# Row-tiled gate matmuls, casting weight loads and an accumulated low part in the recurrent block of a two-layer trunk

## The chip, the cores and the metric

The kernel runs on one core of one Trainium2 chip. The metric is the device time of one execution in microseconds (us), and lower is better. A difference of about 0.2%, here 3.1 us, is what a measurement of this kernel can tell from no change.

## The reference

Two layers work on x, 512 positions by 1024 features, all in float32. Each layer adds half a SwiGLU block, then a mixer, then half a second SwiGLU block; RMSNorm stands ahead of each. The second layer's mixer is a spatial gating unit. The change touches the first layer's mixer alone, the recurrence:

```python
def recurrent_mixer(x, w_in, conv_w, conv_b, gate_a_w, ..., lam, w_out):
    y, r = jnp.split(x @ w_in, 2, axis=-1)          # w_in: 1024 x 2048
    y = jax.nn.gelu(y)
    r = causal_depthwise_conv(r, conv_w, conv_b)    # width 4
    h = rg_lru(r, ...)
    return (y * h) @ w_out                          # w_out: 1024 x 1024

def rg_lru(x, w_a, b_a, w_x, b_x, lam):
    gate_a = sigmoid(block_diag_linear(x, w_a, b_a))   # 16 heads of 64 x 64
    gate_x = sigmoid(block_diag_linear(x, w_x, b_x))
    log_a = -8 * gate_a * softplus(-lam)
    a = exp(log_a)
    bx = x * gate_x * sqrt(-expm1(2 * log_a))
    return associative_scan(a_l * a_r, a_r * b_l + b_r)  # h[t] = a[t] h[t-1] + bx[t]
```

## The kernel before

**Products.** Every matrix product that needs float32 precision is made of three single-pass products in the type fp32r: each operand is split into a high part (the value rounded to fp32r, made by a copy on ScalarE, named `hi` or `whi`) and a low part (value minus high part, made by a subtraction on VectorE, `lo` or `wlo`); high x high, low x high and high x low are summed in PSUM. So one 128x1024 weight tile costs ScalarE one copy and VectorE one subtraction, and TensorE 24 matmuls of 512 columns or their like.

**Steps.** The program is a list of steps (`subs`); a step is one weight tile: its load, its split, its matmuls. A hand-made loop at the end of the kernel emits the steps in order. At each step it emits the split of the tile that is used three steps later (`SPLIT_AHEAD`), then work hooked to this step, in the phases "pre", "mid" and "rest", then as many further weight loads as fit into 10 buffers (`load_more`, `RAW_BUFS`), then the step's matmuls, then hooks of the phases "end" and "late". Every engine runs its own instructions strictly in the order of emission and waits where an operand isn't ready. SyncE's queue carries plain loads; GpSimd's queue carries loads that add onto what is in the buffer.

**The recurrent block.** Features lie on partitions and the 512 positions along the free dimension. It has 20 steps ahead of its output product:

- Eight half steps and four full ones make r, 128 features (c = 0 to 7) at a time. When the last matmul of c is done, `r_post` hooks its work: ScalarE copies r out of PSUM with the conv's last tap, VectorE adds three taps (`taps`), the result `rc` is split (ScalarE `hi`, VectorE `lo`), TensorE makes the gates (`gate`, line 1237 on), ScalarE the two sigmoids out of PSUM and a tanh (`sigmoids`).
- Gates: the 64x64 blocks of two heads stand on the diagonal of a 128x128 weight that is zero elsewhere, one weight for gate a and one for gate x; three matmuls of 128 rows by 512 columns each, so six for one c and 48 in all (lines 248 to 250, tile `gate`).
- Eight full steps make y, 24 matmuls of 512 columns each, with r and y weight tiles 128x8x128 of `rec_w_in`. Meanwhile `plan` sets exp, sqrt, the scan and gelu on ScalarE and VectorE for c = 0 to 4 and then 5 to 7.
- Then the output product, steps of 12 matmuls (tiles A, B, C), reads y*h, which is split like every other left operand. Its `rec_w_out` tiles get sums of blocks by adding loads on GpSimd's queue.

TensorE's matmuls are listed with the weight loads (LDWEIGHTS, engine PEld) that belong to them one for one.

Of the kernel before, what the change touches and what calls it, by code (L numbers as in the profile page):

```python
# [9 lines left out]
F32R = mybir.dt.float32r  # L10
# [4 lines left out]
P = 128  # L15
# [19 lines left out]
RAW_BUFS = 10  # L35
SPLIT_AHEAD = 3
SLOTS = 56
V_AT = 1, 7, 9, 10
WS_AT, WS_MERGE = 90, 8

# [35 lines left out]
def trunk(ctx: ExitStack, tc: tile.TileContext, a: dict, out: bass.AP):  # L76
# [57 lines left out]
    class Raw:  # L134


        halves = False
# [7 lines left out]

        def load(self):
            _, k, c = self.shape
            t = rawp.tile([P, 1024], F32, tag="raw", name=nm("raw"))
            self.v = t[:, : k * c].rearrange("p (k c) -> p k c", k=k)
            live.add(self)  # L150
            self.fetch()
            if self.plus is not None:
                pending.append((now[0] + self.wait, self))
                pending.sort(key=lambda p: p[0])
# [3 lines left out]
                nc.sync.dma_start(out=self.v[:, q, :], in_=self.src[:, q, :])  # L158
# [15 lines left out]
    class Sub:  # L174
# [19 lines left out]
        def split(self, between=None):  # L194

            if self.hi is not None:
                return
            self.add()
            src = self.raw.v
            assert self.tile is None and self.raw.plus is None and self.raw.done == self.at[0]  # L200
# [12 lines left out]
            self.raw.used()  # L213
# [989 lines left out]
    def recurrent(w_in, w_out, norm):  # L1203
        gates = {}

        def load_gate(name, q):
            g = gates[name, q] = slot(name="gw")
            nc.gpsimd.memset(g, 0.0)
            gv = g.rearrange("p (c j) -> p c j", c=4)
            wv = a[f"rec_gate_{name}_w"][0, q * 8 : (q + 1) * 8].rearrange("(c two) i j -> two i c j", two=2)  # L1210
            for two in range(2):
                nc.sync.dma_start(out=gv[two * 64 : (two + 1) * 64, :, two * 64 : (two + 1) * 64], in_=wv[two])

        def split_gate(name, q):
            gates[name, q] = split(gates[name, q])

        at0 = len(subs)
        y0 = at0 + 12
        for n, (name, q) in enumerate((name, q) for q in range(2) for name in ("a", "x")):
            hook(at0 + (-9,-8,-2,-1)[n], "late", lambda name=name, q=q: load_gate(name, q))  # L1220
            hook(at0 + (-3,-2,3,4)[n], "mid", lambda name=name, q=q: split_gate(name, q))

        rc, ga, gx, tl, pr, ym = {}, {}, {}, {}, {}, {}

        def r_post(c, ps):
            n = now[0]
            g = n + (2 if c < 4 or c == 6 else 1)
            v = rc[c] = slot(name="rc")
            hl, pss = [], []
            act(v, ps, AF.Identity, scale=vcol(V_CW + 24 + c), bias=vcol(V_CB + c))  # L1230

            def taps():
                for k in (0, 1, 2):
# [23 lines left out]
            hook(n + 1, "mid", lambda: hl.extend(split(v)))  # L1257
# [57 lines left out]
        plan(1, "late", (exp_, 5, 6, 7), (oma2, 5, 6, 7))  # L1315
        plan(2, "rest", (sqrt, 5, 6, 7))
        plan(2, "late", (gelu, 0, 1, 2), (scan, 5, 6, 7))
# [25 lines left out]
        def mk(c0, post, halves):  # L1343

            raw = raw_of(w_in[:, c0 : c0 + P].rearrange("(k p) c -> p k c", p=P), [P, KD, P])
            st = {}
# [10 lines left out]
            last = lambda: post(st[0])  # L1357
# [310 lines left out]
    def vec_rest():  # L1668

        nc.vector.memset(stage[:V_ROWS, :P], 0.0)  # L1670
        for src, r0, n in rows:
            flat = src.rearrange("h d -> (h d)") if len(src.shape) == 2 else src.rearrange("o h d -> (o h d)")
            nc.gpsimd.dma_start(out=stage[r0 : r0 + n, :P], in_=flat.rearrange("(n p) -> n p", p=P))

    def vec_rest_t():
        ps = aux("vec")
# [146 lines left out]
```

## Time and profile before

| | us |
|---|---|
| median of 3 runs (1559.05 to 1560.93) | 1559.81 |
| the profiled execution | 1559.84 |
| its span, first to last instruction | 1557.0 |
| r steps and the first gates (328.2 to 397.5 of the span, y steps from 383.9 on) | about 69 |
| y steps up to the output product | ends at 430.1 |

The granted TensorE clock is 0.999 over the span. The profiled execution lies 0.03 us from the median, so the sum can be made against it. A row of the timeline reads: start, duration, engine, line, operation, output<-inputs, shapes; in brackets stands idle time of the engine just before, and what ended it. A matmul's duration contains its way through the array, so rows overlap, and the distance from one start to the next is what a matmul takes from TensorE.

### The profile page before, as it was taken

To read this page: it belongs to the slowest core of one execution; us is meant where nothing else is said; L and a number is where in the kernel's file an instruction comes from. 1 tells how busy PE (TensorE), PEld (TensorE's weight loads), DVE (VectorE), ACT (ScalarE), POOL (GpSimd) and SP (SyncE) were. 2 spreads that over 40 slices of the span, in tenths; PEclk is the share of its full clock that TensorE was granted. 3 is DMA by queue.
4 is the path that set the end of the run, shared out by engine and by line. 5 is a ranking of instruction groups with operands and counts; after the bars stand their busy time and mean duration, and the time that the engine had idled before them with its cause. 6 is when DMAs were issued, how large, how long until landed. Compare 5 with 4: busy or idle time off the path is not lost.

```text
span 1557.0 us, 20941 instructions
## 1 busy us (share of the span) xinstructions
PE 1549.4 (100%) x7237; PEld 1314.8 (84%) x7237; DVE 1310.5 (84%) x1792; ACT 1197.0 (77%) x1789; POOL 245.6 (16%) x220
## 2 busy tenths in 40 slices
PE   9999999999999999999999999999999999999998
PEld 7888888898888998888889988888888889888886
DVE  6977789888999787789897877798879997777998
ACT  7877786668778868786787787867887877777866
POOL 2111112300021111112211211122111111111120
PEclk9999999999999999999999999999999999999999
DMA  9988898953395988899987898989978869898994
GB/s 315 189 189 194 187 219 225 225 146 108 99 235 136 190 199 198 186 237 217 233 212 181 201 219 184 223 229 236 233 200 212 203 141 218 195 210 180 242 234 135
DMA packets 275098, 312.09 MB, mean 200 GB/s; under 512 B 117568, under 2 KB 155568, under 8 KB 274992
## 3 DMA queue, kind: packets, MB, share of 16 engines
q1 hardware_dynamic: 220704, 211.59, 47.6%
q0 software_dynamic: 52496, 97.33, 36.9%
q10 hardware_dynamic: 1792, 1.84, 0.4%
q8 instruction: 56, 0.92, 0.2%
q14 instruction: 50, 0.41, 0.1%
HBM read 282.39 MB, written 2.10 MB: 183 GB/s over the span
## 4 chain that ended last, share of the span: by engine, by line
PE 98%; DVE 1%; DMA 1%; issue 0%; ACT 0%; SPq 0%
PE A L484 15%; PE A L483 15%; PE A L485 15%; PE C L483 8%; PE C L485 8%; PE C L484 8%; PE B L484 4%; PE B L485 4%; PE B L483 4%; PE r L248 2%; PE r L250 2%; PE r L249 2%; PE Q L483 1%; PE Q L485 1%; PE Q L484 1%; PE p L963 1%
## 5 line engine op out<-in xcount | busy, mean ns | idle before, releaser
L110 DVE TENSOR_TENSOR wlo<-raw,whi 128x1024 fp32r<-128x1024 f32 (+2 forms) x567 | 651.1, 1152 | 208.8 <-ACT whi L119 203.6
L119 ACT ACTIVATE whi<-raw 128x1024 fp32r<-128x1024 f32 (+2 forms) x567 | 564.3, 1001 | 226.8 <-DVE raw L110 91.6
L483 PE MATMUL A<-whi,hi 128*128 128x512 f32 (+1 forms) x1104 | 420.9, 381 | 0.0
L484 PE MATMUL A<-whi,lo 128*128 128x512 f32 (+1 forms) x1104 | 419.4, 380 | 0.1
L485 PE MATMUL A<-wlo,hi 128*128 128x512 f32 (+1 forms) x1104 | 419.2, 380 | 0.0
L484 PEld LDWEIGHTS A<-whi,lo 128*128 128x128 f32 x1104 | 207.3, 188 | 36.0 <-DVE lo L110 1.0
L483 PEld LDWEIGHTS A<-whi,hi 128*128 128x128 f32 x1104 | 207.2, 188 | 36.0 <-ACT c L119 1.0
L485 PEld LDWEIGHTS A<-wlo,hi 128*128 128x128 f32 x1104 | 207.2, 188 | 35.6
L483 PE MATMUL C<-whi,hi 128*128 128x512 f32 (+1 forms) x608 | 231.5, 381 | 0.0
L484 PE MATMUL C<-whi,lo 128*128 128x512 f32 (+1 forms) x608 | 231.4, 381 | 0.0
L485 PE MATMUL C<-wlo,hi 128*128 128x512 f32 (+1 forms) x608 | 231.3, 380 | 0.0
L161 POOL DMA_DIRECT2D raw<-in_ffn_w_in_dram x100 | 120.7, 1207 | 697.4 <-DVE raw L110 331.5
L161 POOL DMA_DIRECT2D raw<-in_ffn_w_out_dram x73 | 83.8, 1195 | 318.3 <-DVE wlo L110 203.3
L110 DVE TENSOR_TENSOR raw<-raw,raw 128x1024 f32<-128x1024 f32 (+1 forms) x113 | 130.9, 1158 | 1.1
L484 PEld LDWEIGHTS C<-whi,lo 128*128 128x128 f32 x608 | 114.1, 188 | 20.4 <-DVE lo L110 0.4
L485 PEld LDWEIGHTS C<-wlo,hi 128*128 128x128 f32 x608 | 114.1, 188 | 19.9
L483 PEld LDWEIGHTS C<-whi,hi 128*128 128x128 f32 x608 | 114.1, 188 | 19.9
L110 DVE TENSOR_TENSOR lo<-a,hi 128x512 fp32r<-128x512 f32 (+1 forms) x180 | 116.3, 653 | 0.7 <-ACT hi L119 0.7
L119 ACT ACTIVATE c<-A 128x512 f32<-128x512 f32 (+1 forms) x150 | 81.8, 567 | 45.6 <-PE A L485 45.3
L119 ACT ACTIVATE hi<-a 128x512 fp32r<-128x512 f32 (+1 forms) x180 | 105.4, 595 | 14.4 <-DVE a L110 12.8
L484 PE MATMUL B<-whi,lo 128*128 128x512 f32 (+1 forms) x304 | 115.7, 381 | 0.1
L483 PE MATMUL B<-whi,hi 128*128 128x512 f32 (+1 forms) x304 | 115.7, 381 | 0.0
(189 smaller groups left out, 1974.0 us busy)
## 6 DMA issues: line engine op xcount, KB each, us to landing
raw<-in_ffn_w_in_dram SPq DMA_DIRECT2D x143, 512.0 KB, 5.6
raw<-in_ffn_w_out_dram SPq DMA_DIRECT2D x98, 512.0 KB, 6.0
raw<-in_ffn_w_in_dram POOLq DMA_DIRECT2D x76, 512.0 KB, 7.5
raw<-in_ffn_w_out_dram POOLq DMA_DIRECT2D x58, 512.0 KB, 8.6
raw<-in_ffn_w_in_dram SPq DMA_DIRECT2D x48, 384.0 KB, 4.3
raw<-in_sg_w_in_dram SPq DMA_DIRECT2D x20, 512.0 KB, 9.0
raw<-in_ffn_w_in_dram POOLq DMA_DIRECT2D x24, 384.0 KB, 6.2
raw<-in_rec_w_in_dram SPq DMA_DIRECT2D x16, 512.0 KB, 5.1
```

Source lines behind the costliest of these rows:

```text
L110: nc.vector.tensor_tensor(out=o, in0=x, in1=y, op=op)
L119: nc.scalar.activation(out=o, in_=x, func=f, **k)
L161: nc.gpsimd.dma_start(out=self.v, in_=src, accum_op=ALU.add)
L248: nc.tensor.matmul(ps, wh, xh, start=start, stop=False)
L249: nc.tensor.matmul(ps, wh, xl, start=False, stop=False)
L250: nc.tensor.matmul(ps, wl, xh, start=False, stop=stop)
L483: nc.tensor.matmul(ps, zh, wh, start=fresh and i == 0, stop=False, **k)
L484: nc.tensor.matmul(ps, zl, wh, start=False, stop=False, **k)
L485: nc.tensor.matmul(ps, zh, wl, start=False, stop=end, **k)
L963: nc.tensor.matmul(bank_of(half, s), z, (sub.lo if m == 2 else sub.hi)[:, q, :], start=left[2] == "2" and (h, q, m) == (0, 0, 0), stop=lef ...
```

## The change

1. **Gates by row tiles.** One weight of 128 partitions x 128 columns holds gate a and gate x: partitions 0 to 63 hold [a | x] of the first head, partitions 64 to 127 hold [x | a] of the second. A gate's matmul reads 64 partitions and writes 128 PSUM partitions; per c there are still six, three for each half of the partitions, alternating between the halves, and each half has its own PSUM bank. There are two weights in place of four, so two splits in place of four, and no zero fill on GpSimd.
2. **Sigmoids.** Each bank now holds one head's a and x, so a sigmoid covers 64 partitions: four for each c in place of two. The bias of gate x is loaded with its halves swapped (one more small load at the start).
3. **Later gates.** The gates of a c stand 3 or 2 steps after its `r` (`GATE`) where they stood 2 or 1 steps after; c = 2 and 3 come at one place, all others alone. Before, c = 3 and 4 came at one place, and c = 6 and 7. exp, sqrt and the scan move by up to one step.
4. **Casting loads.** For r's c = 4 to 7 and y's c = 0 to 5 the high part is loaded from memory by a load on GpSimd's queue that casts to fp32r (`rawhi`), beside the plain load; ScalarE's copy of these ten tiles goes. Each such tile holds two of the 10 buffers, so loads run fewer tiles ahead.
5. **Accumulated low part.** For y's c = 6 and 7 there is no plain load: ScalarE writes minus the high part to a second buffer (`rawlo`), and an adding load of the same weights onto it makes the low part. VectorE's two subtractions go.
6. **Conv parts.** The high part of `rc` for c = 4 to 7 is a copy on VectorE.

```diff
+GATE = (3, 3, 3, 2, 2, 2, 2, 2)
+OWN_HI = 4
+BELOW = {6: 2, 7: 2}
...
         def load(self):
             _, k, c = self.shape
+            if self.below:
+                self.h, self.l = (rawp.tile([P, 1024], F32R, tag="raw", ...) ... for x in ("rawhi", "rawlo"))
+                live.update(((self, "hi"), (self, "lo")))
+                nc.gpsimd.dma_start(out=self.h, in_=self.src)
+                pending.append((now[0] + self.below, self))
...
+            if self.cast:
+                self.h = rawp.tile([P, 1024], F32R, tag="raw", name=nm("rawhi")).rearrange("p (k c) -> p k c", k=k)
+                live.add((self, "hi"))
+                nc.gpsimd.dma_start(out=self.h, in_=self.src)
...
         def add(self, src):
+            if self.below:
+                act(self.l, f32(self.h), AF.Copy, scale=-1.0)
+                nc.gpsimd.dma_start(out=self.l, in_=self.src, accum_op=ALU.add)
+                return
...
+            if self.raw.cast:
+                self.hi = self.raw.h
+                ...
+                tt(self.lo, src, f32(self.hi), ALU.subtract)
+                self.raw.used()
+                return
...
-            g = n + (2 if c < 4 or c == 6 else 1)
+            g = n + GATE[c]
...
             def gate():
-                for name in "ax":
-                    pg = bank("gate")
-                    wh, wl = gates[name, c // 4]
-                    cs = slice((c % 4) * P, (c % 4 + 1) * P)
-                    mm3(pg, wh[:, cs], wl[:, cs], hl[0], hl[1], True, True)
-                    pss.append(pg)
+                pss.extend(bank("gate") for _ in range(2))
+                cs = slice((c % 4) * P, (c % 4 + 1) * P)
+                for m in range(3):
+                    for two in range(2):
+                        rows = slice(two * 64, (two + 1) * 64)
+                        nc.tensor.matmul(pss[two], gates[c // 4][m == 2][rows, cs], hl[0][m == 1][rows, :],
+                                         start=m == 0, stop=m == 2)
...
             def sigmoids():
-                for dst, brow in ((ga, V_GA), (gx, V_GX)):
-                    dst[c] = slot(name="g")
-                    act(dst[c], pss.pop(0), AF.Sigmoid, bias=vcol(brow + c))
+                for dst, brow, n in ((ga, V_GA, 0), (gx, V_GX, 1)):
+                    g = dst[c] = slot(name="g")
+                    for two in range(2):
+                        o = (two ^ n) * 64
+                        act(g[two * 64 : (two + 1) * 64], pss[two][o : o + 64], AF.Sigmoid, bias=vcol(brow + c)[o : o + 64])
...
+                if c < OWN_HI:
+                    act(hi, v, AF.Copy)
+                else:
+                    nc.vector.tensor_copy(hi, v)
+                tt(lo, v, f32(hi), ALU.subtract)
...
-        plan(-2, "rest", (exp_, 0, 1, 2, 3, 4), (oma2, 0, 1))
+        plan(-1, "rest", (exp_, 0, 1, 2, 3, 4), (oma2, 0, 1))
...
-        while loaded < n and len(live) < RAW_BUFS:
+        while loaded < n and len(live) < RAW_BUFS - raws[loaded].cast:
```

On TensorE, around the gates of c = 0, the kernel before has (`gate` is the PSUM bank, first operand the weight, second what streams):

```order
L250 MATMUL r_3267<-zh_3086,wlo_3179 128x256
L248 MATMUL gate_3463<-hi_3394,hi_3112 128x512
L249 MATMUL gate_3463<-lo_3395,hi_3112 128x512
L250 MATMUL gate_3463<-hi_3394,lo_3113 128x512
L248 MATMUL gate_3467<-hi_3394,hi_3134 128x512
L249 MATMUL gate_3467<-lo_3395,hi_3134 128x512
L250 MATMUL gate_3467<-hi_3394,lo_3135 128x512
L248 MATMUL r_3332<-zh_3058,whi_3209 128x256
```

and the changed kernel has, one half step later:

```order
L279 MATMUL r_3323<-zh_3082,wlo_3201 128x256
L1273 MATMUL gate_3481<-hi_3379,hi_3110 128x512
L1273 MATMUL gate_3482<-hi_3379,hi_3110 128x512
L1273 MATMUL gate_3481<-lo_3380,hi_3110 128x512
L1273 MATMUL gate_3482<-lo_3380,hi_3110 128x512
L1273 MATMUL gate_3481<-hi_3379,lo_3111 128x512
L1273 MATMUL gate_3482<-hi_3379,lo_3111 128x512
L277 MATMUL r_3512<-zh_3054,rawhi_2936 128x512
```

The count is the same; the two banks alternate, and the gates stand between the last half step and the first full one.

On GpSimd's queue, where the kernel before has four zero fills and then adding loads of `rec_w_out`, the changed kernel has, after eight more rows of the kind of the first two:

```order
L166 DMA rawhi_3642<-in_rec_w_in_dram 128x8x128
L166 DMA rawhi_3713<-in_rec_w_in_dram 128x8x128
L155 DMA rawhi_3783<-in_rec_w_in_dram 128x8x128
L155 DMA rawhi_3846<-in_rec_w_in_dram 128x8x128
L178 DMA rawlo_3784<-in_rec_w_in_dram 128x8x128
L178 DMA rawlo_3847<-in_rec_w_in_dram 128x8x128
L180 DMA raw_3910<-in_rec_w_out_dram 128x2x512 x2
L180 DMA raw_4048<-in_rec_w_out_dram 128x2x512
```

So the adding load of y's last low part (`rawlo_3847`) is followed on its queue by those of `rec_w_out`.

On ScalarE, at the end of the recurrence (`gate` to `g` is a sigmoid, `tl` a sqrt, `y` a gelu), the changed kernel has:

```order
L122 ACTIVATE tl_3835<-tl_3835 128x512
L122 ACTIVATE tl_3894<-tl_3894 128x512
L122 ACT_TABLE_LOAD
L122 ACTIVATE y_3940<-r_3786 128x512
L122 ACTIVATE y_3942<-r_3849 128x512
L122 ACTIVATE y_3944<-r_3912 128x512
L122 ACTIVATE rawlo_3847<-rawhi_3846 128x1024
L122 ACTIVATE hi_3992<-a_838_3959 128x512
```

The kernel before has the same three gelus there, followed by the `whi` copy of y's c = 6. What moved in is the negated copy for y's c = 7, which can't start before the gelus are through.

More of the change, by code (lines that the diff above doesn't have):

```diff
@@ L147, in load @@
             _, k, c = self.shape
+            if self.below:
+                self.h, self.l = (rawp.tile([P, 1024], F32R, tag="raw", name=nm(x)).rearrange("p (k c) -> p k c", k=k)
+                                  for x in ("rawhi", "rawlo"))
+                live.update(((self, "hi"), (self, "lo")))
+                nc.gpsimd.dma_start(out=self.h, in_=self.src)
+                pending.append((now[0] + self.below, self))
+                pending.sort(key=lambda p: p[0])
+                return
             t = rawp.tile([P, 1024], F32, tag="raw", name=nm("raw"))
@@ L198, in split @@
             self.add()
+            if self.raw.below:
+                self.hi, self.lo = self.raw.h, self.raw.l
+                return
             src = self.raw.v
+            if self.raw.cast:
+                self.hi = self.raw.h
+                _, k, c = src.shape
+                self.lo = wp.tile([P, 1024], F32R, tag="wlo", name=nm("wlo")).rearrange("p (k c) -> p k c", k=k)
+                tt(self.lo, src, f32(self.hi), ALU.subtract)
+                self.raw.used()
+                return
             assert self.tile is None and self.raw.plus is None and self.raw.done == self.at[0]
@@ L1204, in recurrent, with load_gate, split_gate @@
         gates = {}
[L1206 to L1208 removed]
+        def load_gate(q):
+            g = gates[q] = slot(name="gw")
             gv = g.rearrange("p (c j) -> p c j", c=4)
[L1210 to L1215, printed above, removed]
+            for n, name in enumerate("ax"):
+                wv = a[f"rec_gate_{name}_w"][0, q * 8 : (q + 1) * 8].rearrange("(c two) i j -> two i c j", two=2)
+                for two in range(2):
+                    o = (two ^ n) * 64
+                    nc.sync.dma_start(out=gv[two * 64 : (two + 1) * 64, :, o : o + 64], in_=wv[two])
+        def split_gate(q):
+            gates[q] = split(gates[q])
         at0 = len(subs)
         y0 = at0 + 12
[L1219 to L1221 removed]
+        for q in range(2):
+            hook(at0 + (-9, -2)[q], "late", lambda q=q: load_gate(q))
+            hook(at0 + (-3, 3)[q], "mid", lambda q=q: split_gate(q))
         rc, ga, gx, tl, pr, ym = {}, {}, {}, {}, {}, {}
@@ L1345, in mk @@
             raw = raw_of(w_in[:, c0 : c0 + P].rearrange("(k p) c -> p k c", p=P), [P, KD, P])
+            raw.cast = not halves
+            raw.below = BELOW.get(c0 // P, 0)
             st = {}
@@ L1355, in mm_of, with last @@
                 return mm
-            last = lambda: post(st[0])
+            def last():
+                live.difference_update(((raw, "hi"), (raw, "lo")))
+                post(st[0])
             if not halves:
@@ L1672, in vec_rest @@
             flat = src.rearrange("h d -> (h d)") if len(src.shape) == 2 else src.rearrange("o h d -> (o h d)")
-            nc.gpsimd.dma_start(out=stage[r0 : r0 + n, :P], in_=flat.rearrange("(n p) -> n p", p=P))
+            v = flat.rearrange("(n p) -> n p", p=P)
+            if r0 == V_GX:
+                for o in (0, 64):
+                    nc.gpsimd.dma_start(out=stage[r0 : r0 + n, o : o + 64], in_=v[:, 64 - o : 128 - o])
+            else:
+                nc.gpsimd.dma_start(out=stage[r0 : r0 + n, :P], in_=v)
     def vec_rest_t():
```

17 lines of the change are left out of this document (12 added, 5 removed).

## The prediction

> **What bounds the kernel now.** I read the page first: its engines and its chain.
>
> ```profile
> span 1557.0 us, 20941 instructions
> PE 1549.4 (100%) x7237; PEld 1314.8 (84%) x7237; DVE 1310.5 (84%) x1792; ACT 1197.0 (77%) x1789; POOL 245.6 (16%) x220
> ...
> PE 98%; DVE 1%; DMA 1%; issue 0%; ACT 0%; SPq 0%
> ```
>
> TensorE is busy throughout and carries 98% of the chain. Next the view by stretches: r's full steps and y up to 430.1, then the output product.
>
> ```profile
> 356.60:397.50 40.90, 40.90 (x182) 33.87 (x182) 35.15 (x47) 34.71 (x50) 2.41 (x2) 1.00 0.41 104
> 397.50:430.10 32.60, 32.60 (x145) 27.03 (x144) 31.24 (x46) 23.13 (x33) 3.20 (x3) 1.00 0.35 98
> 430.10:470.00 39.90, 39.90 (x189) 33.28 (x188) 37.69 (x52) 29.09 (x50) 8.88 (x8) 1.00 0.94 223
> ```
>
> The columns are the stretch, its length, then PE, PEld, DVE, ACT and POOL, clock, DMA share, GB/s. TensorE never stops here, at a granted clock of 1.00. So a microsecond taken from VectorE, ScalarE or DMA buys nothing by itself; only TensorE's own work, or a new wait of TensorE, changes the time. VectorE, with 31.24 of 32.60 us, is the engine nearest to making it wait.
>
> **Change part by part. Gates on TensorE.** The first gate in the timeline:
>
> ```profile
> 350.95 0.40 PE L248 MATMUL gate<-hi,hi 128*128 128x512 f32 x1
> 351.18 0.40 PE L249 MATMUL gate<-lo,hi 128*128 128x512 f32 x1
> ...
> 352.33 0.28 PE L248 MATMUL r<-zh,whi 128*128 128x256 f32 x1
> ```
>
> Six matmuls take 352.33 - 350.95 = 1.38 us, 0.23 each. Eight gates are 8 x 1.38 = 11.0 us. After, two half-height matmuls on different partitions can run side by side. If they do, a gate streams three times 0.23 = 0.69 us, and 24 x 0.23 = 5.5 us go. No row has two side by side; the bounds are 0 and 5.5, and I take 5.5, since they share neither rows of the array nor a bank.
>
> What entering and leaving the other shape costs, one place shows: near the start a transpose of 8 rows stands between full-height warm-up matmuls, which start 0.42 us apart there, at about half the later pace.
>
> ```profile
> 1.67 1.91 PE L1660 MATMUL warm<-warm 128*128 128x512 bf16 x4
> 3.51 0.27 PE L1665 MATMUL vec<-ident,first_gain 8*128 8x8 f32 x1
> ...
> 2.10 0.15 PEld L1660 LDWEIGHTS <-warm 128*128 128x128 bf16 x1 [0.28 <-issue]
> 2.52 0.15 PEld L1660 LDWEIGHTS <-warm 128*128 128x128 bf16 x1 [0.28 <-issue]
> 3.51 0.18 PEld L1665 LDWEIGHTS vec<-ident,first_gain 8*128 8x128 f32 x1 [0.84 <-issue]
> 3.71 0.13 PEld L1660 LDWEIGHTS <-warm 128*128 128x128 bf16 x2
> ...
> 22.11 0.87 PE e L294 x8
> ```
>
> Full-height weight loads start one matmul early (2.10, 2.52: 0.42 apart, the stream of one matmul). The fourth warm-up matmul starts at 1.67 + 3 x 0.42 = 2.93 and has streamed by 3.35; the small weight load starts only at 3.51, and the next full one only at 3.71. So weights aren't loaded ahead across the change of shape, and the round trip took 3.71 - 3.35 = 0.36 us with next to nothing streamed, plus the second weight load. At full pace I halve it, 0.18, and add 0.11 for that load (eight transposes, each with its load, took 0.87): 0.29; unhalved it is 0.47. I take 0.33, near the halved end, because the array's part goes with its pace. The second half's weights come 0.11 us after the first's, which staggers the end: 0.11 more. There are seven places after (c = 2 and 3 share one): 7 x 0.44 = 3.1 us; bounds 0 (no drain, no stagger) and 7 x 0.58 = 4.1.
>
> Net on TensorE: -5.5 + 3.1 = **-2.4 us**, from -5.5 to -1.4 where the halves pair.
>
> The Trainium skill, "TensorEngine Tiling (Array Packing)", section "Key Properties", says that changing the tiling mode drains TensorE; the trace agrees in this one place (0.36 us at half the pace). The Trainium skill, "TensorE: Matmul & The Clock Gate", section "Part 3: Packing small matmuls — row/col tiling", has packed matmuls start about 4 ns apart; no run here shows it, and by it the stagger of 0.77 us in all would go, giving -3.1.
>
> **ScalarE.** Its timeline over one round, and the gelus at the end:
>
> ```profile
> 359.08 1.06 ACT L119 ACTIVATE whi<-raw 128x1024 fp32r<-128x1024 f32 x1
> 360.03 1.27 ACT L119 ACTIVATE g<-gate,vec 128x512 f32<-128x512 f32 x2
> 361.17 0.74 ACT L119 ACTIVATE tl<-g,lru_c 128x512 f32<-128x512 f32 x1
> 361.78 0.65 ACT L119 ACTIVATE hi<-rc 128x512 fp32r<-128x512 f32 x1
> 362.33 0.78 ACT L119 ACTIVATE rc<-r,vec 128x512 f32<-128x512 f32 x1
> ...
> 410.44 1.58 ACT L119 ACTIVATE y<-r 128x512 f32<-128x512 f32 x3
> ```
>
> A sigmoid costs (361.17 - 360.03) / 2 = 0.57, a `whi` 0.95, a `hi` 0.55. A 64-partition sigmoid streams as many columns, so I price it like a full one (bounds 0.29 and 0.57). Up to the three gelus: 16 more sigmoids +9.1, ten `whi` copies -9.5, four `hi` -2.2, one negated copy +0.95: -1.7 us. So the gelus end not at 410.44 + 1.58 = 412.0 but near 410.3; as the gates come later I allow 411 +- 2, and the negated copy for y's last tile ends near **412**.
>
> **The accumulated low part, the edit with a wait.** That copy releases the adding load; TensorE needs its result in the y step of c = 7:
>
> ```profile
> 425.14 0.39 PE L250 MATMUL r<-zh,wlo 128*128 128x512 f32 x1
> ...
> q0 software_dynamic: 816, 1.57, 8.4%
> ...
> raw<-in_rec_w_out_dram SPq DMA_DIRECT2D x10, 512.0 KB, 3.9
> raw<-in_rec_w_in_dram SPq DMA_DIRECT2D x8, 512.0 KB, 4.1
> raw<-in_rec_w_out_dram POOLq DMA_DIRECT2D x5, 512.0 KB, 7.4
> ```
>
> (DMA view, 318 to 430.) First use of this low part is at 425.14, after the change 425.1 - 2.4 = 422.7. Adding loads land in 7.4 us, but with rows of 2 KB; these have 512 bytes, four times the packets. On the plain queue that costs 0.2 us (4.1 against 3.9). On the adding queue a packet takes 8.4% x 16 x 112 us / 816 = 0.18 us of an engine; if small ones took as long, 768 more on 16 engines add 8.9. Bounds 7.6 and 16.3; I take 9, nearer the plain rows because the bytes are the same. 412 + 9 = 421: 1.7 us to spare, cost 0; without that cover up to 412 + 16.3 - 422.7 = 5.6 us of TensorE waiting. Behind it on GpSimd's queue stand the `rec_w_out` additions; their readers have the slack of three steps.
>
> **VectorE, the loads.** VectorE loses two subtractions of 1.2 us and two gate splits and gains four one-input copies, whose nearest row is 0.48, at most a subtraction's 0.68:
>
> ```profile
> L110 DVE TENSOR_TENSOR wlo<-raw,whi 128x1024 fp32r<-128x1024 f32 x453 | 550.8, 1220 | 164.1 <-ACT whi L119 158.9 <-DMA raw<-in_sg_w_out_dram 3.6
> L113 DVE TENSOR_SCALAR xn<-x,rt 128x512 f32<-128x512 f32 x6 | 2.6, 482 | 0.1
> ...
> 439.77 0.68 DVE L110 TENSOR_TENSOR lo<-a,hi 128x512 fp32r<-128x512 f32 x1
> 441.23 0.39 PE L484 MATMUL C<-whi,lo 128*128 128x512 f32 x1
> ```
>
> In the y stage that is 4 x 0.48 - 2.4 = -0.5 us or, at 0.68, +0.3. The tightest meeting behind it has 441.23 - 440.45 = 0.8 us, and an earlier TensorE uses this up; so a gain far over 2.4 us would partly turn into waiting here. At 2.4 I put it at nothing, and up to 2 us if nothing on VectorE moves up.
>
> Twelve casting loads and two adding ones bring some 6 MB more into these stretches at 98 to 104 GB/s, where the next one runs at 223 without stopping TensorE: nothing. GpSimd has the time (2.4 and 3.2 us busy in these stretches). `rec_w_out`'s first load moves:
>
> ```profile
> 357.60 64.13 SPq L158 DMA_DIRECT2D raw<-in_rec_w_out_dram  x10
> ```
>
> from 357.6, some 70 us before its use at 430.1, to three steps (of 24 x 0.23 = 5.5 us) before its split, against 3.9 to land: hidden.
>
> **The sum.** -2.4 + 0 + 0 on the profiled execution's 1559.84, which equals the median within 0.03: **1557.4 us**.
>
> **Rivals.**
>
> *A, the shapes change without a drain.* For it: the delay was seen once, at half the pace, in a warm-up that nothing hurried. Against: the weight loads at 3.51 and 3.71 themselves. Then only the stagger stays, -5.5 + 0.8 = -4.7 (1555.1), and c = 7's low part, needed at 420.4, lands at 421, so some 0.4 comes back: 1555.5.
>
> *B, the halves don't run together.* For it: no row shows two matmuls overlapping by more than their way through the array. Then nothing is saved and the seven round trips are paid, 7 x 0.33 = +2.3, up to 7 x 0.47 = +3.3: about 1562.5, slower. It decides whatever else holds, as soon as the second half's start comes 0.23 us after the first's.
>
> *C, the adding load comes late.* Its place is y's c = 7; it decides from a landing after 422.7, that is over 10.7 us or a ScalarE over 2 us behind my reckoning. At 16.3 us it costs 5.6: 1559.8 - 2.4 + 5.6 = 1563.0; in the middle 1560. For it: only a guess stands for small adding packets. Against: the plain rows.
>
> **Chances.** Forecast (-1.4 to -3.5) 0.42, A 0.28, B 0.12, C 0.18. Within 0.2% (3.1 us) is what a measurement of this kernel can't tell from no change. Faster by more: nearly all of A (0.27) and a seventh of the forecast (0.06): 0.33. Slower by more: over half of B (0.07) and of C (0.10): 0.17. Same: 0.50. The forecast's own range is 1556.3 to 1558.4; to hold 8 in 10 it goes down into A, 1554.6, and up through most of C and half of B, 1562.3.
>
> **What would show it.** In the profile after: the second half's matmul of a gate starts at most 0.12 us after the first's, and the six take about 0.8 us where they took 1.38 (else B). The gap from the last full-height matmul to the first gate and back adds some 0.3 us (none: A). ScalarE's gelus end at 411 +- 2. The last `rawlo` lands within 10 us and TensorE doesn't wait in y's c = 7 (else C). TensorE is first to reach the output product, near 427.7. A wait of TensorE on a conv part (`hi` or `lo` of `rc`), a gate's bank or a `rawhi` would prove my cover wrong.

## The result

| | us |
|---|---|
| before, median of 6 runs (1558.81 to 1560.93) | 1559.06 |
| after, median of 6 runs (1570.06 to 1576.33) | 1570.90 |
| forecast | 1557.4 (1554.6 to 1562.3) |

The changed kernel takes 1.0078 times as long, 95% interval 1.0064 to 1.0093: some 12 us slower, outside the range. Its profiled execution took 1570.06 us with a span of 1568.2, 11.2 us longer than the span before.

### The profile page after: what moved, and what is told of

Read it like the earlier page. It is cut to its first block, busy times and chain, and to the rows that moved or that the text cites. A ratio compares the mean times of both kernels' runs of the same rounds, so it can differ in the third digit from the quotient of the medians.

```text
span 1568.2 us, 20979 instructions
## 1 busy us (share of the span) xinstructions
PE 1549.4 (99%) x7237; PEld 1310.0 (84%) x7237; DVE 1308.7 (83%) x1792; ACT 1196.3 (76%) x1789; POOL 256.9 (16%) x231
## 3 DMA queue, kind: packets, MB, share of 16 engines
q10 hardware_dynamic: 1792, 1.84, 0.5%
## 4 chain that ended last, share of the span: by engine, by line
PE 69%; DVE 2%; DMA 1%; issue 1%; ACT 0%; POOL 0%; DVEq 0%; POOLq 0%; ACTq 0%
PE A L513 12%; PE A L512 12%; PE A L514 12%; PE C L513 7%; PE C L514 7%; PE C L512 7%; PE B L513 3%; PE B L512 3%; PE B L514 3%; PE Q L513 1%; PE Q L512 1%; PE Q L514 1%; DMA raw<-in_rec_w_out_dram 1%; PE e L323 1%; DVE wlo L113 1%
## 5 line engine op out<-in xcount | busy, mean ns | idle before, releaser
L113 DVE TENSOR_TENSOR wlo<-raw,whi 128x1024 fp32r<-128x1024 f32 (+2 forms) x555 | 636.4, 1150 | 222.0 <-ACT whi L122 215.7
L122 ACT ACTIVATE whi<-raw 128x1024 fp32r<-128x1024 f32 (+2 forms) x555 | 551.6, 1000 | 243.3 <-DVE raw L113 93.1
L514 PE MATMUL B<-wlo,hi 128*128 128x512 f32 (+1 forms) x304 | 115.7, 380 | 0.0
```

What stands on the lines that cost most here:

```text
L113: nc.vector.tensor_tensor(out=o, in0=x, in1=y, op=op)
L122: nc.scalar.activation(out=o, in_=x, func=f, **k)
L514: nc.tensor.matmul(ps, zh, wl, start=False, stop=end, **k)
```

## The profile after: one new wait

The head of the page, and what TensorE waited for (us in total, times, longest):

```profile
span 1568.2 us, 20979 instructions
PE 1549.4 (99%) x7237; PEld 1310.0 (84%) x7237; DVE 1308.7 (83%) x1792; ACT 1196.3 (76%) x1789; POOL 256.9 (16%) x231
...
PE C L512 <- ACT hi L122: 9.2, 1, 9.2
PE r L279 <- DMA rawlo<-in_rec_w_in_dram: 1.4, 1, 1.4
```

TensorE's busy time is the same to 0.1 us, the span isn't. The view by stretches, with the borders used before:

```profile
356.60:397.50 40.90, 40.90 (x191) 30.75 (x190) 36.60 (x51) 39.12 (x55) 5.49 (x6) 1.00 0.82 155
397.50:430.10 32.60, 31.21 (x139) 25.50 (x138) 27.64 (x41) 22.85 (x32) 4.54 (x4) 1.00 0.69 162
430.10:470.00 39.90, 30.46 (x131) 24.56 (x130) 30.19 (x44) 19.22 (x29) 10.65 (x9) 0.87 0.96 228
```

In the first stretch TensorE gets 191 matmuls done where it did 182: the pairing pays. In the third it does 131 where it did 189, and its mean granted clock falls to 0.87. The loss lies at one place there, in TensorE's timeline:

```profile
422.73 0.39 PE L278 MATMUL r<-zl,rawhi 128*128 128x512 f32 x1
424.51 0.50 PE L279 MATMUL r<-zh,rawlo 128*128 128x512 f32 x1 [1.39 <-DMA rawlo<-in_rec_w_in_dram]
...
429.63 0.39 PE L512 MATMUL A<-whi,hi 128*128 128x512 f32 x1
...
440.29 0.39 PE L514 MATMUL A<-wlo,hi 128*128 128x512 f32 x1
449.83 0.79 PE L512 MATMUL C<-whi,hi 128*128 128x512 f32 x1 [9.16 <-ACT hi L122]
450.91 0.79 PE L513 MATMUL C<-whi,lo 128*128 128x512 f32 x1 [0.28 <-DVE lo L113]
...
453.79 0.39 PE L514 MATMUL C<-wlo,hi 128*128 128x512 f32 x1
```

A matmul here takes 0.23 us from start to start. From 440.29 to 449.83 are 9.54 us, 9.3 too much. The next eight starts, to 453.79, take 3.96 us where 8 x 0.23 = 1.84 would do, 2.1 more: 0.28 is a short wait for VectorE, and the rest comes from TensorE's slow pace after the long wait (0.42 to 0.43 from start to start, at a granted clock of 0.51 from 449.83 to 453.56). With 1.55 us at 424.51, TensorE comes to the output product at 429.63, only 0.5 us earlier than before (430.13). So -0.5 + 9.3 + 2.1 = +10.9 of the 11.2 us lie before 454.

The chain of waits over this place shows what `hi` had waited for (start, length, what):

```profile
416.52 1.87 DMA raw<-in_rec_w_out_dram
418.39 11.47 issue
...
430.61 14.28 DMA raw<-in_rec_w_out_dram
...
445.00 1.06 ACT whi L122
```

and GpSimd's own timeline why the addition at 430.61 came so late:

```profile
415.63 1.55 POOL L178 DMA_DIRECT2D rawlo<-in_rec_w_in_dram  x1 [13.51 <-ACT rawlo L122]
416.52 1.87 POOL L180 DMA_DIRECT2D raw<-in_rec_w_out_dram  x1
429.88 2.43 POOL L180 DMA_DIRECT2D raw<-in_rec_w_out_dram  x2 [11.49 <-DVE wlo L113]
```

GpSimd issues in order. The adding load for y's c = 7 waits 13.5 us there for ScalarE's negated copy. Behind it, at 416.52, goes the addition onto P5's tile for ci = 0 (`P5` is the second product of the output; ci tells which half of the features of y*h it sums over, where the expectation of e1 says column half). Next in the queue is the *second* addition onto that same tile, which must wait until the tile is split; behind that stands the first addition for ci = 1, which had nothing to wait for. It goes out at 430.61 with its neighbour, lands 14.28 us later, and ScalarE, VectorE and TensorE follow it one after another. In the kernel before, this addition stood ahead of the second one for ci = 0. Its GpSimd timeline has it at 387.91, and the second one for ci = 0 at 421.75:

```profile
387.91 1.20 POOL L161 DMA_DIRECT2D raw<-in_rec_w_out_dram  x1 [19.47 <-DVE rc L116]
421.75 1.20 POOL L161 DMA_DIRECT2D raw<-in_rec_w_out_dram  x1 [32.63 <-DVE wlo L110]
```

## Experiments

All times are medians; ratios are to the kernel before, run on the same chip in the same set. That kernel's own median differs by up to 1.6 us from set to set (1559.73 to 1561.37), so ratios are compared across sets. "Start" is TensorE's first matmul of the output product in the profiled execution; it was 430.13 before and 429.63 after. These executions come to r's first matmul at different times, from 328.6 to 329.6 (before 329.06, after 329.38), so starts compare to about half a microsecond. The profiled executions of e3, e5, e12 and e13 took 2.9 to 5.7 us longer than their medians; TensorE waits 2.7 to 3.6 us in them beyond 500 us, outside the changed part.

| run | median | ratio, 95% interval | start |
|---|---|---|---|
| e1 | 1562.34 | 1.0016 (1.0006 to 1.0026) | 429.64 |
| e2 | 1560.85 | 1.0014 (0.9996 to 1.0032) | 430.04 |
| e3 | 1558.85 | 0.9988 (0.9972 to 1.0004) | 427.86 |
| e4 | 1568.12 | 1.0055 (1.0037 to 1.0073) | 437.57 |
| e5 | 1560.87 | 0.9999 (0.9982 to 1.0015) | 427.60 |
| e6 | 1564.32 | 1.0023 (1.0008 to 1.0038) | 430.22 |
| e7 | 1567.59 | 1.0032 (1.0016 to 1.0047) | 427.47 |
| e8 | 1558.71 | 0.9984 (0.9970 to 0.9998) | 427.19 |
| e9 | 1560.23 | 0.9996 (0.9982 to 1.0011) | 427.27 |
| e10 | 1585.31 | 1.0147 (1.0121 to 1.0173) | 427.87 |
| e11 | 1559.47 | 1.0001 (0.9987 to 1.0016) | 429.28 |
| e12 | 1561.46 | 1.0000 (0.9980 to 1.0019) | 429.84 |
| e13 | 1558.57 | 0.9982 (0.9969 to 0.9995) | 427.96 |

### The place in GpSimd's queue: e1, e2, e7

e1 moves one addition one step forward, past the one that waits.

```diff
+    raws[92].wait = 1            # P5, ci = 1: emitted 1 step after its load, not 2
```

> The changed kernel with one addition of rec_w_out moved: the add onto the tile of P5 for the second column half (ci = 1) is emitted one step earlier, ahead of the second add onto the tile of P5 for ci = 0, which waits on GpSimd's queue for that tile's split. Theory Q (place in GpSimd's queue): in the changed kernel the add for ci = 1 had its plain load at 418.4 and was issued only at 430.6 because it stood behind the other, which waited 11.5 us for VectorE; ahead of it, it goes out near 417.5, lands by 432, and the wait of 9.2 us of TensorE at C with the slow clock behind it goes. Left are -0.5 us at the start of the output product (429.6 against 430.1): 1559.3 us. Theory L (late landing under load): the adds land late because the DMA engines are full (share 0.96); two adds at once land in 14.3 us, the one for ci = 0 then lands near 432 in place of 427.2 and everything behind it in ScalarE's queue moves by 5 us: 4 to 5 us of TensorE's wait stay, 1563 to 1566 us.

Measured: 1562.34; the ratio falls from 1.0078 to 1.0016, so 0.0062 x 1560 = 9.7 of the 12 us are back. Both additions go out together at 416.37, and TensorE's waits are:

```profile
416.37 3.10 POOL L180 DMA_DIRECT2D raw<-in_rec_w_out_dram  x2
...
PE r L279 <- DMA rawlo<-in_rec_w_in_dram: 1.6, 1, 1.6
PE C L512 <- ACT hi L122: 0.6, 1, 0.6
PE C L513 <- DVE lo L113: 0.6, 1, 0.6
```

Theory Q holds. The add for ci = 0 landed at 427.3 as before, not at 432, so theory L's mechanism isn't there, though the time lies between the two forecasts, with 1.2 us of waits at C that neither named. (The plain load "at 418.4" in the expectation was misread: 418.39 is the end of GpSimd's instruction in the chain; the plain load had landed at 415.4.)

e2 also lets the addition for ci = 0 pass the adding load for y's c = 7.

```diff
+    raws[89].wait, raws[92].wait = 0, 1
```

> As the run before, and the add onto the tile of P5 for ci = 0 is emitted ahead of the adding load of y's last low part, so it no longer stands behind ScalarE's negated copy (415.6 us). Theory Q: it goes out near 404 to 405, when its plain load (issued at 398.8) has landed, and no add shares the engines with y's last low part at 415.6; that one then lands a little sooner than in 8.8 us and the wait of 1.4 us in y's last step shrinks: 1558.0 us (1557.5 to 1559.3). Theory L: the landing is set by the load on the engines between 410 and 430 us, where as many bytes flow as before: no better than the run before, 1559.3 or more.

Measured: the same as e1 within the intervals. In its trace the waits at C are 0.2 us in all, so what e1 had left there came from the block by ScalarE's negated copy; y's last low part still costs 1.6, against the expectation.

e7 is the counter-test. It takes e3 (below), where ScalarE blocks nothing, and puts only the place in the queue back.

```diff
-BELOW = {6: 2, 7: 2}
+BELOW = {}
+    raws[92].wait = 3
```

> As e3 (no accumulated low parts, GpSimd's queue not blocked by ScalarE), but the add of rec_w_out for P5, ci = 1, is emitted later, behind the second add for ci = 0, where it stood in the changed kernel. Theory Q: the place alone costs: the second add for ci = 0 goes out at 428.2 when its split is done, the one for ci = 1 at 428.9 behind it, and with both in flight it lands 9 to 14 us later, 438 to 443, where TensorE wants its split at 440: a wait of 1 to 5 us more than in e3, 1560 to 1564 us. Rival (only the block by ScalarE's negated copy up to 415.6 counts): as e3, 1558.9 us.

Measured: 1567.59; by the ratios 0.0044 x 1560 = 6.9 us above e3, more than expected. From its timelines of GpSimd, ScalarE and TensorE's waits:

```profile
427.84 3.67 POOL L180 DMA_DIRECT2D raw<-in_rec_w_out_dram  x3 [21.25 <-DVE wlo L113]
...
439.56 1.06 ACT L122 ACTIVATE whi<-raw 128x1024 fp32r<-128x1024 f32 x1 [7.32 <-DMA raw<-in_rec_w_out_dram]
...
PE C L512 <- ACT hi L122: 5.9, 1, 5.9
```

One addition behind one that waits is enough for a wait of 5.9 us and the half pace behind it. With e1, which takes the loss back by the place alone, this settles its cause.

### Without the accumulated low parts: e3, e8, e5

```diff
-BELOW = {6: 2, 7: 2}
+BELOW = {}                  # e3;  e8: {6: 2};  e5: {6: 2, 7: 1} and e2's line
```

> The changed kernel with y's c = 6 and 7 as casting tiles like c = 0 to 5: no negated copy, no adding load, two more subtractions on VectorE. Theory Q: GpSimd's queue isn't blocked until 415.6; the add for ci = 0 goes out near 405, its split and the second add follow at its place on VectorE (about 422), and the add for ci = 1 goes out at once behind, near 423, lands near 434, in time for its use at 440: the wait of 9.2 us is gone, and the wait of 1.4 us at y's last step too. TensorE reaches the output product at 430.13 - 2.3 = 427.8; VectorE has 2.4 us more to do in a stretch where it is busy 31 of 32.6 us, which costs 0 to 2: 1557.5 to 1559.5 us. Theory L: the loads of rec_w_out still come some 60 us later than before the change, since each casting tile holds two of ten buffers, and TensorE waits 3 us or more for ci = 1: over 1560.5.

Measured: 1558.85, start at 427.86, as theory Q said. The order mends itself: a casting tile gives one of its two buffers back at its split, three steps ahead of its matmuls, where an accumulated one keeps both to its last matmul; so P5's tiles load earlier, and the add for ci = 1 stands ahead of the second one again (416.79). Three matmuls at C start 1.7 us late together (0.6 + 0.6 of it idle), for VectorE, which has no gap from 427.83 to 440.6, in the chain:

```profile
427.83 1.42 DVE a L113 x4
...
439.87 0.70 DVE lo L113
440.61 0.50 PE C L513
```

> The changed kernel with the accumulated low part for y's c = 6 alone, whose adding load is issued at 400.6 and is needed only near 417; c = 7 is a casting tile. The last adding load for y and its block of GpSimd's queue up to 415.6 are gone, and the add for P5, ci = 1, stands ahead of the second one for ci = 0 without being moved. Theory: TensorE reaches the output product at 427.9 and VectorE has one subtraction (1.2 us) less than in e3, so of its 1.2 us of waits at C at most 0.3 stay: 1557.8 us. Rival (VectorE isn't what takes the gain back in e3): as e3, 1558.9 us.

Measured: 0.9984 (0.9970 to 0.9998), by the ratio some 2.5 us faster than the kernel before, and the lowest ratio here of a version that leaves no work out. The gain isn't secure: the interval just allows it, it lies under the 0.2% named at the start, the lowest runs of the set are 0.7 us apart (1557.65 and, before, 1558.39), and e9 below, the same work, has 0.9996. From the changed kernel it differs in the one entry of `BELOW`. Its waits, and the stretch after 450, which still loses (TensorE was busy all of it before):

```profile
PE C L513 <- DVE lo L113: 0.4, 1, 0.4
...
450.00:500.00 50.00, 49.42 (x234) 40.78 (x233) 46.73 (x69) 41.55 (x72) 7.22 (x6) 1.00 0.80 192
```

> Both additions of rec_w_out early as in e2, and the negated copy of y's c = 7 a step earlier, ahead of the last sigmoids on ScalarE. Its casting load was issued at 387.9 and needs about 5.5 us, so the copy can run near 398 and its adding load lands near 410, long before its use at 422.5: the 1.6 us of TensorE's wait at r are gone and so is the wait of GpSimd's queue. TensorE reaches the output product at 427.9 as in e3, and VectorE has two subtractions (2.4 us) less than there, so the waits at C (0.6 + 0.6 us) go too. Theory (the pairing's 2.3 us are taken back by this queue and by VectorE alone): 1557.5 us (1557.0 to 1558.3). Rival: ScalarE is the tighter engine there, its exp, gelus and what follows move by 1.05 us and the first left operands come late: 1558.5 to 1560.

Measured: no difference from before. Start at 427.60 and no wait at all until 450, as the theory said, but then the waits come at 453 and 457 (0.5 us each): VectorE had idled 3.6 us at 447.6 for ScalarE, which had idled 6.5 us for an addition of `rec_w_out`. Less work for VectorE alone doesn't help when the additions come late.

### What the gates need: e4, e6, e12, e9, e11

e4 takes all casting and accumulating loads away.

```diff
+BELOW = {}
-            raw.cast = not halves
+            raw.cast = False
```

> Row-tiled gates, split sigmoids, their later places and the conv parts on VectorE, without any casting or accumulating load: loads and buffers as before the change, and ScalarE makes all twelve whi copies again. If the pairing's gain is what the trace shows (six matmuls and the two changes of shape in 1.09 us against 1.38, eight times, -2.2) and ScalarE has room: 1557.5. Rival: ScalarE has no room. 32 sigmoids of 64 partitions at 0.71 against 16 at 0.57 are +13.6, four hi copies less -2.2, so its gelus would end at 412 + 11.4 = 423.4 in place of 412; it had 5.5 us idle behind them, so some 6 us remain and TensorE waits for y's banks or for the first left operands: 1560 to 1564.

Measured: 1568.12; the rival holds, and more than it said. TensorE waits for `whi` copies that stand behind sigmoids on ScalarE:

```profile
400.07 2.81 ACT L122 ACTIVATE g<-gate,vec 64x512 f32<-64x512 f32 x4
...
416.13 1.58 ACT L122 ACTIVATE y<-r 128x512 f32<-128x512 f32 x3
417.58 1.07 ACT L122 ACTIVATE whi<-raw 128x1024 fp32r<-128x1024 f32 x1
...
PE r L277 <- ACT whi L122: 5.2, 2, 3.4
```

e6 is e4 with two full sigmoids:

```diff
-                        act(g[two * 64 : (two + 1) * 64], pss[two][o : o + 64], AF.Sigmoid, ...)
+                    act(dst[c], pss.pop(0), AF.Sigmoid, bias=vcol(brow + c))
```

> As e4 (no casting or accumulating loads), but with two sigmoids over 128 partitions for each c in place of four over 64; so gate a and gate x are exchanged for every second head, which changes the computed values and no other work. Theory (in e4 ScalarE's +13.6 us for the sigmoids made TensorE wait 5.7 us and slowed its clock): ScalarE has 16 x 0.57 = 9.1 us for them as before the change, TensorE doesn't wait, and the output product starts at 430.1 - 2.3 = 427.8: 1557.5 us. Rival (something else in e4 costs, such as the later gates or the conv parts on VectorE): over 1562 us, with the same waits on whi as in e4.

Measured: 1564.32, the start 7.3 us earlier than e4's, yet 2.4 us later than the 427.8 expected. So the sigmoids explain most of e4, not all. VectorE idles 4.5 us before 413.80 for a `whi` that stands behind the gelus; in the changed plan the last scans stand behind that subtraction. The moved places rely on the casting loads.

e12 is e8 with the gates and sigmoids of the kernel before:

```diff
-                pss.extend(bank("gate") for _ in range(2))
-                ...
+                for name in "ax":
+                    pg = bank("gate")
+                    wh, wl = gates[name, c // 4]
+                    mm3(pg, wh[:, cs], wl[:, cs], *hl[0], True, True)
```

> As e8, with the gates as before the change: two zero-filled weights, six matmuls of full height for a c, two sigmoids over 128 partitions. The later places of the gates, the casting loads, the one accumulated low part and the conv parts on VectorE stay. TensorE has 8 x 1.38 us for the gates in place of 8 x 1.09 to 1.14 (some 2.2 us more), ScalarE 16 x 0.57 in place of 32 x 0.71 (13.6 us less). Theory V (in e8 the pairing's 2.2 us are taken back behind 430 us by VectorE and the loads): TensorE comes 2.2 us later to the output product and waits less there, so the time is at most 0.7 us over e8's: 1558.7 to 1559.4 us. Rival (the pairing is what makes e8 faster than before, and its whole gain arrives): 1560.9 us.

Measured: 1.0000 (0.9980 to 1.0019), 2.5 us above e8 by the ratios, with intervals that overlap. It points to the rival: the start is at 429.84, 2.6 us later than e8's, and between 450 and 500 it is busy as little (49.35 of 50 us, e8 49.42), so theory V, by which the later start would be made up by fewer waits, doesn't hold there. By these medians the pairing's gain arrives, and the rest of the change gains nothing without it.

e9 is e8 with each half's three matmuls in a row:

```diff
-                for m in range(3):
-                    for two in range(2):
+                for two in range(2):
+                    for m in range(3):
```

> As e8, but the six matmuls of a gate are put in another order: the three of the first half of the partitions, then the three of the second, in place of alternating halves. Everything else is the same. Theory (side by side means pairs next to each other): only the third of the first half and the first of the second are neighbours on different partitions, so a gate streams five times 0.23 us in place of three: 8 x 0.47 = +3.7 us on TensorE, of which up to 1.2 us fall into time that TensorE waits for VectorE behind 438 us anyway: 1561.2 to 1562.4 us. Rival (the two halves can't overlap across different steps of the sum): six times 0.23, +5.5 us on TensorE, 1563 to 1564 us. Rival (TensorE reorders, the order doesn't matter): as e8, 1558.7 us.

Measured: as e8 within the intervals, and the start as well (427.27). The rival that had the least behind it holds. In e9's timeline the rows still come in pairs:

```profile
373.90 0.50 PE L1273 MATMUL gate<-hi,hi 64*128 64x512 f32 x2
374.24 0.40 PE L1273 MATMUL gate<-lo,hi 64*128 64x512 f32 x2
374.48 0.40 PE L1273 MATMUL gate<-hi,lo 64*128 64x512 f32 x2
```

> As e8, with two small changes whose effects are read apart in the trace. First the order of the four sigmoids: now each differs from the one ahead of it only in the partitions it reads or only in those it writes, where both or the written ones changed each time. If only the read ones matter for the 0.71 us, the starts are 0.71, 0.57, 0.71 apart or the other way round if only the written ones matter; if either matters, or the number of partitions itself is the cause, all stay at 0.71. Second, c = 0 and 1 get their gates in one place, so there are six changes of shape and back in place of seven: TensorE gains 0.39 us. Time: as e8 less 0.4, or the same, since VectorE takes it back behind 438 us: 1558.3 to 1558.7 us.

```diff
-GATE = (3, 3, 3, 2, 2, 2, 2, 2)
+GATE = (3, 2, 3, 2, 2, 2, 2, 2)
+                for dst, brow, n, two in ((ga, V_GA, 0, 0), (gx, V_GX, 1, 1), (ga, V_GA, 0, 1), (gx, V_GX, 1, 0)):
```

Measured: 1559.47, start at 429.28. The sigmoids' starts stay 0.70 to 0.71 us apart whichever side changes. The common place for c = 0 and 1 saves its change of shape, but TensorE then stops twice behind gates that come in pairs (before 356.81 and 370.29, idle for 1.0 and 0.8 us), for nothing that the profile shows. That loss isn't explained.

### Buffers and VectorE: e10, e13

e10 is e8 with `RAW_BUFS = 11` and `SLOTS = 54`.

> As e8, with 11 buffers for weight tiles in place of 10 (and 54 of the other slots in place of 56). Theory (what e8 still loses behind 430 us, 0.67 + 1.09 us more than before the change, comes from the loads of rec_w_out that start late since casting tiles hold two buffers: an add was issued at 430.8 and ScalarE waited 4.5 us for it until 444.7): each load starts a tile earlier, ScalarE's wait at 444.7 shrinks by 2 us or more and TensorE's waits behind 438 us by half or more: 1557.9 us (1557.3 to 1558.5). Rival (VectorE's own work is the bound behind 430 us): as e8, 1558.7 us. If the 54 slots are too few, some engine waits on a slot and it is slower.

Measured: 1585.31. It waits at other stages too (8.8 us at one A alone); whether 54 slots are too few or the additions move everywhere isn't separated, so it tells nothing of theory against rival.

```diff
+                if self.raw.once:            # y's c = 2, 3, 4, 5, 7
+                    self.lo = self.hi
+                    self.raw.used()
+                    return
```

> As e8, without the subtraction that makes the low part for y's c = 2, 3, 4, 5 and 7: the high part is read in its place, so these five products are computed from other values, and VectorE has 5 x 1.2 = 6 us less to do between 386 and 421 us; TensorE's work and all loads stay. Theory V (VectorE is what takes the pairing's gain back): it reaches the left operands of the output product earlier, the waits at C near 438 us (0.5 us) and at the transposes near 465 us (0.5 + 0.45 us) go: 1557.6 us, 1 us under e8. Rival L (the additions of rec_w_out, loaded late, are what is waited for there): VectorE only waits longer for ScalarE's whi copies, and the time stays at e8's 1558.7 us.

Measured: 0.9982 (0.9969 to 0.9995), lowest run 1556.10 against e8's 1557.65. In its trace TensorE has no wait from 400 to 500, which is theory V:

```profile
400.00:450.00 50.00, 50.00 (x223) 41.38 (x222) 45.55 (x68) 32.91 (x45) 10.92 (x9) 1.00 0.90 212
450.00:500.00 50.00, 50.00 (x238) 41.76 (x237) 46.52 (x68) 42.22 (x73) 7.22 (x6) 1.00 0.76 189
```

The ratios of e13 and e8 differ by 0.0002, or 0.3 us, within their uncertainty; so theory V rests on the stretches of one execution each, and e5 shows that late additions bind as well.

## Why the prediction was wrong

**TensorE: right.** The first gate after, and the row that follows:

```profile
354.03 0.28 PE L279 MATMUL r<-zh,wlo 128*128 128x256 f32 x1
354.24 0.50 PE L1273 MATMUL gate<-hi,hi 64*128 64x512 f32 x2
354.58 0.40 PE L1273 MATMUL gate<-lo,hi 64*128 64x512 f32 x2
354.81 0.39 PE L1273 MATMUL gate<-hi,lo 64*128 64x512 f32 x2
355.13 0.50 PE L277 MATMUL r<-zh,rawhi 128*128 128x512 f32 x1
355.47 0.39 PE L278 MATMUL r<-zl,rawhi 128*128 128x512 f32 x1
```

The two halves start 3 to 4 ns apart, so rival B falls, and so does the stagger of 0.11. The two changes of shape cost 0.40 here: from start to start 0.21, 0.34, 0.23 (the pairs) and 0.32, 0.34 (back), against 0.12 and 4 x 0.23 streamed. At the places behind full steps they cost 0.42. 0.33 + 0.11 = 0.44 had been taken, so the sum is right by two errors that cancel: the change of shape costs more than 0.33, and the stagger is nothing. From r's first matmul to the output product TensorE takes 101.07 us before and 98.56 in e3, e5, e7, e8 and e13, which have no wait in between: -2.5, as 24 x 0.227 - 7 x 0.42 gives, where -2.4 was forecast. Rival A falls. (The -3.1 that the prediction names without the stagger is -3.2 by its own terms, -5.5 + 7 x 0.33.) The Trainium skill, "TensorE: Matmul & The Clock Gate", section "Part 3: Packing small matmuls — row/col tiling", has packed matmuls start about 4 ns apart; the trace agrees (3 to 4 ns).

**ScalarE: a term mis-sized.** "I price it like a full one" (0.57, bounds 0.29 and 0.57) was too low, though it was the upper bound:

```profile
395.75 2.81 ACT L122 ACTIVATE g<-gate,vec 64x512 f32<-64x512 f32 x4
398.58 0.72 ACT L122 ACTIVATE tl<-g,lru_c 128x512 f32<-128x512 f32 x1
...
412.69 1.58 ACT L122 ACTIVATE y<-r 128x512 f32<-128x512 f32 x3
414.14 1.07 ACT L122 ACTIVATE rawlo<-rawhi 128x1024 fp32r<-128x1024 f32 x1
```

(398.58 - 395.75) / 4 = 0.71 each, so 32 of them cost 4.5 us more than priced. Each lasts no longer than a full one (0.68 to 0.69); full ones overlap by 0.12 and these don't. The gelus end at 414.3, beyond 411 +- 2, and the negated copy at 415.2 in place of 412.

**The adding load: right, and too late all the same.** It landed 8.8 us after its issue (forecast 9, rival C from 10.7), but the copy that releases it ended 3.2 us late, so TensorE waited 1.4. This is rival C's place by its second condition ("ScalarE over 2 us behind my reckoning").

**GpSimd's queue: the step that failed.** "Behind it on GpSimd's queue stand the `rec_w_out` additions; their readers have the slack of three steps." The slack was counted for each addition alone from its place in the program. It wasn't asked what each of them waits for in the queue. The first waited for ScalarE (to 415.63), the second for VectorE's split of the very tile that the first had filled (to 429.88), and the third, which waited for nothing, stood behind both. That the later loads of `rec_w_out` are "hidden" failed with it: the plain load of this tile was (landed at 415.4), but the order of the additions follows from when the loads are emitted, and two buffers for each tile had moved that by six steps for ci = 1 and also for ci = 0. The wait, 9.3 + 2.1 us, was on no list: "GpSimd has the time" was true of its busy time (4.5 of 32.6 us) and beside the point.

**VectorE: the place right, the size open.** The prediction saw the tightest meeting at C, with 0.8 us, and took 0 for it, at most 2 us. In e3, where nothing else is in the way, it is at C that 1.7 us go; but e3 has two subtractions, 2.4 us of VectorE's work, more than the changed kernel. With one subtraction more (e8) TensorE idles 0.4 us there. With none (e5, which starts at 427.60) it doesn't wait there, only 0.5 us at a later C (453). So the 0 held for this meeting, and what the next ones cost wasn't in the sum.

**The chances.** "Slower by more", 0.17, doesn't follow from the rivals' own figures: B at about 1562.5 and C at up to 1563.0 lie within or only just beyond 3.1 us of 1559.84.

Put together for the profiled execution: -2.5 for the gates, +0.3 because TensorE came to r's first matmul that much later, +1.7 for y's last low part, +11.4 for the queue, in all +10.9 of +11.2. With the queue mended and one accumulated part less, e8 has the ratio that the forecast named for the changed kernel, 1557.4 / 1559.84 = 0.9984; its waits behind the start weren't counted there, and its gain isn't secure, so this is partly luck.

## What to carry over

On a queue that issues in order, ask of each entry what it waits for, and look for entries with nothing to wait for that stand behind one that has; busy time says nothing about this. When a change makes transfers start later, print the new order on every queue and redo the waits in it, since the emission time of a load also sets the place of what is hooked to it. And price a narrower instruction by start-to-start distances: the chip may lose the overlap that neighbours had.

## What was not expected of the hardware

- **TensorE runs the two halves out of program order.** In e9 the three matmuls of one half stand ahead of the three of the other, and still they run in pairs, the second of a pair 10 ns behind the first (3 to 4 ns when they alternate). So the strict order of emission, told above of every engine, doesn't hold for these pairs. The Trainium skill, on the page and in the section named above, says that matmuls start strictly in program order; here the measurement differs.
- **Neighbouring activations over 64 partitions, of which each starts at another partition than the one ahead, don't overlap** (0.71 from start to start; 0.57 over 128), whether the partitions read, the ones written or both change (e11). A smaller number of partitions alone doesn't do it: the first of four, behind a 128-partition instruction that starts at the same partition, does overlap in the profile after (it starts at 400.17, the negated copy ahead of it ends at 399.21 + 1.05 = 400.26). That points to the change of the first partition; two neighbours of 64 partitions with the same start weren't run. The Trainium skill, "ScalarE: Activation LUTs", section "What ACT_TABLE_LOAD costs", gives 280 + 0.833 N ns for one with a bias column, by which an estimate for 512 columns is 0.707 us, and an overlap of 0.09 us for neighbours. In this trace these start 0.71 us apart, and that overlap is missing.
- **Adding loads of `rec_w_out` in flight together land one by one, some 4 us apart**, whatever their issue times. From the records of e10, issue and landing:

```
426.82  436.88
429.65  440.89
435.93  444.89
436.65  448.90
440.61  452.90
```

Alone, one lands after some 7 us (before: 387.91 to 395.07); three at once keep the last for 14 (e7: 429.38 to 443.38). Behind a `rawlo` load the distance is shorter (in the changed kernel 424.46, then 427.24). So the time to land depends on how many are in flight, and the 7.4 us of the profile before was the median of five loads, at most two at a time. In the unchanged part of the program, too, single executions show such a load landing late (16.2 us at 904 us in e12, where TensorE then waits 3.6 us). Whether this is what makes their times scatter wasn't tested.
